# Even and odd tokens in separate halves: a hybrid decoder block whose products read their streamed operand interleaved

## The chip, the cores and the metric

The kernel runs on one core of one Trainium2 chip. The metric is the device time of one execution in microseconds. Three runs of the kernel before the change are given, with their median; one further execution was taken by the hardware profiler.

## The reference

One decoder layer over 256 tokens of width 1024 in float32: two attention branches of 8 heads of 64 (MoBA with rotated queries and keys, FoX with a forget gate), merged by per-channel sigmoid gates, an output projection, then a gated feed-forward part with a causal convolution over three tokens. With 256 tokens MoBA has one block, so both branches are plain causal attention.

```python
h = rms_norm(x, attn_norm_g)
proj = h @ w_in                       # q, k, v of both branches, forget logits, 2 x 1024 gate logits
o_a = merge_heads(moba_attention(qa, ka, va))
o_b = merge_heads(forgetting_attention(qb, kb, vb, log_f))
br_a = o_a @ w_branch_moba            # 512 -> 1024
br_b = o_b @ w_branch_fox             # 512 -> 1024
gates = sigmoid(g_logit + b_gate)
merged = gates[:, :, 0] * br_a + gates[:, :, 1] * br_b
x = x + merged @ w_out                # 1024 -> 1024
h2 = rms_norm(x, ffn_norm_g)
u, g = split(h2 @ w_ffn_up)           # 1024 -> 2 x 2816
g = causal_depthwise_conv(g, ffn_conv_w, ffn_conv_b)
x = x + (silu(g) * u) @ w_ffn_down    # 2816 -> 1024
```

## The kernel before, in words

Everything lies transposed: channels on the 128 partitions, the 256 tokens along the free dimension. A tile such as `oh` is 128 x 8 x 256: eight blocks of 128 channels, each a row of 256 tokens per partition, 4 bytes each.

**Products in three terms.** Every large product is made of reduced fp32 operands (`F32R`). A weight is split into `whi` (its rounded copy, ScalarE, L124) and `wlo` (the rest, VectorE, L125); an activation likewise into a high tile and a low tile. Each 128x128 piece of weight then takes three matmuls: high weight by high activation, high weight by low activation, low weight by high activation. In the products behind attention, and in the gates, the weight piece is the stationary operand and the activation the moving (streamed) one: 256 columns, one for each token, and 256 columns of a PSUM bank as the result.

**The stages, in order on TensorE** (its order is written out by hand):

1. The projections to queries, keys and values (`project`, L222). There the activations `xh` and `xl` are stationary, and 512 columns of weight are streamed. Attention's smaller work (transposes L395, `values` L406) and the eight gate chunks (`gate`, which calls `twin`, L430 to L432, with `xh` and `xl` streamed) are woven between them.
2. `values` makes each pair of heads' output in PSUM and splits it into `oh` (ScalarE, L408) and `ol` (VectorE, L409).
3. The branch products (`wb`, L527 to L529) stream `oh` and `ol`. Their results are multiplied by the gates and added (L533, L534), and split into `mh` (L535) and `ml` (L536), which take the buffers of `xh` and `xl`.
4. The output product (`wo`, L553 to L555) streams `mh` and `ml`; the sum with x is split into `hh` (L561) and `hl` (L562), in the buffers of `oh` and `ol`. The squares for the second norm go to GpSimd and back (L566 to L569, L580).
5. Feed-forward: `up(f)` for 22 chunks streams `hh` and `hl` through `twin` (L430 to L432). It scales the result (L583), runs the convolution (L587 to L589), the SiLU (ScalarE, L590) and the product with u (VectorE, L591) into the halves `sl` and `av` of a work tile, and splits that into `ah` (L595) and `al` (L596), in buffers named qA, qB and kA. `down(p)` (L614 to L616) streams `ah` and `al` of two chunks; it runs one pair of chunks behind `up`. The last one adds x (L620) and sends the output (L621).

Weights come on SyncE's queue, 1 MB at a time, into three `raw` buffers (`load`, L120); `use` asks for the split of a half chunk five halves ahead, in six pairs of `whi` and `wlo`.

Of the kernel before, what the change touches and what calls it, by code (L numbers as in the profile page):

```python
# [8 lines left out]
F32 = mybir.dt.float32  # L9
F32R = mybir.dt.float32r  # L10
BF16 = mybir.dt.bfloat16
AF = mybir.ActivationFunctionType
ALU = mybir.AluOpType
# [5 lines left out]
S = 256  # L19
NT = 2  # L20
D = 1024
KT = D // P
# [19 lines left out]
def decoder_block(ctx, tc, a, out):  # L42
    nc = tc.nc
# [139 lines left out]
    def rsqrt_mean(dst, ss, n, shape, tag):  # L183

        w = T([P, 3] + shape, tag, 2)
        v, y, t = w[:, 0], w[:, 1], w[:, 2]
        nc.vector.tensor_scalar(v, ss, 1.0 / n, EPS, op0=ALU.mult, op1=ALU.add)
        nc.scalar.activation(t, v, AF.Ln)
        nc.scalar.activation(y, t, AF.Exp, scale=-0.5)
        nc.vector.scalar_tensor_tensor(t, v, -0.5, y, op0=ALU.mult, op1=ALU.mult)  # L190
        nc.vector.tensor_tensor(t, t, y, op=ALU.mult)
        nc.vector.scalar_tensor_tensor(dst, t, 1.5, y, op0=ALU.add, op1=ALU.mult)

    rs = T([P, NT], "rs")
    rope = []
# [162 lines left out]
    oh = T([P, KT, S], "oh", 1, F32R)  # L358
    ol = T([P, KT, S], "ol", 1, F32R)
# [39 lines left out]
    def values(br, pair):  # L399
        pT = probs.pop((br, pair))  # L400
        op = bank()
        for i, c in enumerate((slice(0, 256), slice(256, 384))):
            for j in range(2):
                o = HD * j
                vc = br * W4 + (2 * pair + j) * HD
                nc.tensor.matmul(op[o:o + HD, i * P:S], V[:, i, vc:vc + HD], pT[:, j, c], start=(i == 0), stop=(i == 1))  # L406
        b = 4 * br + pair
        nc.scalar.activation(oh[:, b], op[:, 0:S], AF.Copy)  # L408
        nc.vector.tensor_tensor(ol[:, b], op[:, 0:S], oh[:, b].bitcast(F32), op=ALU.subtract)  # L409


    gates = lt[:, :, S:].rearrange("p k (b t) -> p k b t", b=2)
# [5 lines left out]
            nc.tensor.matmul(rp[:, t * P:(t + 1) * P], rs[:, t:t + 1].to_broadcast([P, P]), ident, start=True, stop=True)  # L418
        nc.vector.tensor_copy(rsB, rp[:, 0:S])

    def twin(kind, c, dst, mh, ml):

        for h in range(2):
            wh, wl = use((kind, c), h)
            for i in range(2):
                o = dst[:, i * S:(i + 1) * S]
                for k4 in range(4):
                    k = 4 * h + k4
                    w = slice(k4 * 256 + i * P, k4 * 256 + (i + 1) * P)
                    nc.tensor.matmul(o, wh[:, w], mh[:, k], start=(k == 0 and i == 0), stop=False)  # L430
                    nc.tensor.matmul(o, wh[:, w], ml[:, k], start=False, stop=False)  # L431
                    nc.tensor.matmul(o, wl[:, w], mh[:, k], start=False, stop=(k == KT - 1 and i == 1))  # L432

    def gate(c):
        gp = bank()
# [81 lines left out]
    mh = T([P, KT, S], "xh", 1, F32R)  # L517
    ml = T([P, KT, S], "xl", 1, F32R)
    for c in range(4):
        bp = banks()  # L520
        for br in range(2):
            wh, wl = use(("wb", c), br)
            for j in range(2):
                o = bp[j][:, br * S:(br + 1) * S]
                for k in range(4):
                    w = slice(k * 256 + j * P, k * 256 + (j + 1) * P)
                    nc.tensor.matmul(o, wh[:, w], oh[:, 4 * br + k], start=(k == 0), stop=False)  # L527
                    nc.tensor.matmul(o, wh[:, w], ol[:, 4 * br + k], start=False, stop=False)  # L528
                    nc.tensor.matmul(o, wl[:, w], oh[:, 4 * br + k], start=False, stop=(k == 3))  # L529
        for j in range(2):  # L530
            b = 2 * c + j
            m2 = T([P, 2, S], "sq", 2)
            nc.vector.tensor_tensor(m2, bp[j].rearrange("p (b t) -> p b t", b=2), gates[:, b], op=ALU.mult)  # L533
            nc.vector.tensor_tensor(m2[:, 0], m2[:, 0], m2[:, 1], op=ALU.add)  # L534
            nc.scalar.activation(mh[:, b], m2[:, 0], AF.Copy)  # L535
            nc.vector.tensor_tensor(ml[:, b], m2[:, 0], mh[:, b].bitcast(F32), op=ALU.subtract)  # L536


    hh = T([P, KT, S], "oh", 1, F32R)
    hl = T([P, KT, S], "ol", 1, F32R)  # L540
    acc = [bank() for _ in range(4)]
    x1 = xT
    sqs = T([P, S], "sqs")
    for c in range(4):
        for h in range(2):
            wh, wl = use(("wo", c), h)
            j = 2 * (c % 2) + h
            for i in range(2):
                o = acc[j][:, i * S:(i + 1) * S]
                for k4 in range(4):  # L550
                    k = 4 * (c // 2) + k4
                    w = slice(k4 * 256 + i * P, k4 * 256 + (i + 1) * P)
                    nc.tensor.matmul(o, wh[:, w], mh[:, k], start=(k == 0 and i == 0), stop=False)  # L553
                    nc.tensor.matmul(o, wh[:, w], ml[:, k], start=False, stop=False)  # L554
                    nc.tensor.matmul(o, wl[:, w], mh[:, k], start=False, stop=(k == KT - 1 and i == 1))  # L555
            if c >= 2:
                xx = x1[:, 2 * j:2 * j + 2]
                nc.vector.tensor_tensor(xx, acc[j].rearrange("p (b t) -> p b t", b=2), xx, op=ALU.add)
                for b in (2 * j, 2 * j + 1):
                    g = col(C_G2 + b)  # L560
                    nc.scalar.activation(hh[:, b], x1[:, b], AF.Copy, scale=g)  # L561
                    nc.vector.scalar_tensor_tensor(hl[:, b], x1[:, b], g, hh[:, b].bitcast(F32), op0=ALU.mult, op1=ALU.subtract)  # L562
                sq = T([P, 2, S], "sq", 2)
                nc.scalar.activation(sq, xx, AF.Square)
                if j == 0:
                    nc.gpsimd.tensor_tensor(sqs, sq[:, 0], sq[:, 1], op=ALU.add)  # L566
                else:
                    nc.gpsimd.tensor_tensor(sqs, sqs, sq[:, 0], op=ALU.add)
                    nc.gpsimd.tensor_tensor(sqs, sqs, sq[:, 1], op=ALU.add)  # L569
# [5 lines left out]

    def up(f):
        up_ = bank()
        twin("wu", f, up_, hh, hl)
        if f == 0:
            nc.tensor.matmul(sp[:, 0:S], ones, sqs, start=True, stop=True)  # L580
            rsqrt_mean(rs2, sp[:, 0:S], D, [S], "pT")
        ev = T([P, 2, S], "sq", 2)
        nc.vector.tensor_tensor(ev, up_.rearrange("p (b t) -> p b t", b=2), rs2[:, None, :].to_broadcast([P, 2, S]), op=ALU.mult)  # L583
        u, g = ev[:, 0], ev[:, 1]
        w = T([P, 3, S], "s", 3)
        cv, sl, av = w[:, 0], w[:, 1], w[:, 2]
        nc.scalar.activation(cv, g, AF.Identity, scale=col(C_CW + 2 * NF + f), bias=col(C_CB + f))  # L587
        nc.vector.scalar_tensor_tensor(cv[:, 1:], g[:, 0:S - 1], col(C_CW + NF + f), cv[:, 1:], op0=ALU.mult, op1=ALU.add)
        nc.vector.scalar_tensor_tensor(cv[:, 2:], g[:, 0:S - 2], col(C_CW + f), cv[:, 2:], op0=ALU.mult, op1=ALU.add)  # L589
        nc.scalar.activation(sl, cv, AF.Silu)  # L590
        nc.vector.tensor_tensor(av, u, sl, op=ALU.mult)  # L591
        if f % 2 == 0:
            acts[f // 2] = T([P, 4, S], ("qA", "qB", "kA")[f // 2 % 3], 1, F32R)
        ah, al = acts[f // 2][:, f % 2], acts[f // 2][:, 2 + f % 2]
        nc.scalar.activation(ah, av, AF.Copy)  # L595
        nc.vector.tensor_tensor(al, av, ah.bitcast(F32), op=ALU.subtract)  # L596
# [4 lines left out]
    def down(p):  # L601
        ac = acts.pop(p)
        last = p == NF // 2 - 1
        w2 = [use(("wd", p), h) for h in range(2)]
        order = [(h, d) for d in ((0, 1), (2, 3), (4, 5), (6,), (7,)) for h in range(2)] if last else [(h, (d,)) for h in range(2) for d in range(KT)]
        for h, ds in order:
            wh, wl = w2[h]
            ah, al = ac[:, h], ac[:, 2 + h]
            for d in ds:
                b = 4 if d == 7 else d // 2  # L610
                c = d % 2 if d < 6 else 0
                o = acc[b][:, c * S:(c + 1) * S]
                w = slice(d * P, (d + 1) * P)
                nc.tensor.matmul(o, wh[:, w], ah, start=(p == 0 and h == 0 and c == 0), stop=False)  # L614
                nc.tensor.matmul(o, wh[:, w], al, start=False, stop=False)  # L615
                nc.tensor.matmul(o, wl[:, w], ah, start=False, stop=(last and h == 1 and d == ds[-1]))  # L616
            if last and h == 1:
                n = len(ds)
                y = yy[:, ds[0]:ds[0] + n]
                nc.vector.tensor_tensor(y, acc[b][:, 0:n * S].rearrange("p (b t) -> p b t", b=n), x1[:, ds[0]:ds[0] + n], op=ALU.add)  # L620
                nc.sync.dma_start(out[:, ds[0]:ds[0] + n], y)  # L621
# [75 lines left out]
```

## Time and profile before

| | us |
|---|---|
| three runs | 377.33, 384.51, 383.91 |
| median | 383.91 |
| profiled execution: span from the first to the last instruction | 376.7 |
| TensorE busy in it | 368.5 (98%) |
| VectorE busy | 286.6 (76%) |
| ScalarE busy | 228.0 (61%) |
| GpSimd busy | 16.8 (4%) |
| HBM read | 66.60 MB, 180 GB/s over the span |

The profiled execution has no time of its own besides its span; the fastest run lies 0.6 us above that span and the median run 7.2 us. The granted TensorE clock is 0.999 of full speed.

A row of a group gives line, engine, operation, the tiles it writes and reads, shapes and count, then busy time, the mean duration of one in ns, and the idle time before it with what ended it. Matmuls are pipelined: one lasts longer than the step from its start to the next one's start, and it is the step that counts. The timeline gives start and duration in us.

### The profile page before, as it was taken

The page shows a single profiled execution, that of the slowest core. Times are in us where ns is not written, and L with a number is a line of the kernel's source. Part 1 is how long each engine was busy: PE and PEld are TensorE (multiplying, and loading weights), DVE is VectorE, ACT ScalarE, POOL GpSimd, SP SyncE. Part 2 cuts the span into 40 slices and gives each one's busy share as a digit, 9 for nine tenths or more (in the row PEclk, how much of TensorE's full clock was granted, in tenths as well). Part 3 has the DMA queues.
Part 4 walks back from the last instruction along what each step waited for, and adds up shares of the span by engine and source line. Part 5 has one row for each costly group of instructions (what it writes and reads, how often), then busy time and mean ns, then how long its engine had stood idle before and what let it go on. Part 6 is the DMA issues. An engine that isn't in the chain of part 4 may idle for free.

```text
span 376.7 us, 7085 instructions
## 1 busy us (share of the span) xinstructions
PE 368.5 (98%) x2893; PEld 347.0 (92%) x2893; DVE 286.6 (76%) x504; ACT 228.0 (61%) x382; POOL 16.8 (4%) x19
## 2 busy tenths in 40 slices
PE   7999999999999999999999999999999999999995
PEld 3788887879999999999999999999999999999995
DVE  3979989899997664786787978677686867778653
ACT  4947698659957794545578756464655545455520
POOL 2420000000000000000070000000000000000000
PEclk9999999999999999999999999999999999999999
DMA  7966521735265433545554645564455455545003
GB/s 310 384 254 225 224 113 34 303 130 208 110 215 176 171 113 118 218 161 182 217 172 164 225 171 179 211 222 175 171 216 208 162 197 217 202 151 210 2 0 111
DMA packets 11232, 68.11 MB, mean 181 GB/s; under 512 B 1464, under 2 KB 2624, under 8 KB 3648
## 3 DMA queue, kind: packets, MB, share of 16 engines
q1 hardware_dynamic: 10896, 66.60, 48.7%
q10 hardware_dynamic: 304, 1.06, 0.7%
q8 instruction: 22, 0.36, 0.4%
q14 instruction: 10, 0.08, 0.1%
HBM read 66.60 MB, written 1.06 MB: 180 GB/s over the span
## 4 chain that ended last, share of the span: by engine, by line
PE 79%; ACT 8%; DVE 7%; DMA 3%; issue 1%; POOLq 0%; POOL 0%; SPq 0%; ACTq 0%
PE bank L432 13%; PE bank L430 13%; PE bank L431 13%; PE bank L222 10%; PE bank L616 5%; PE bank L615 5%; PE bank L614 5%; DVE wlo L125 2%; ACT whi L124 2%; PE bank L527 2%; PE bank L528 2%; PE bank L529 2%; DMA lead<-in_lead 2%; ACT qA L273 1%; DMA raw<-in_wg 1%; PE bank L554 1%
## 5 line engine op out<-in xcount | busy, mean ns | idle before, releaser
L125 DVE TENSOR_TENSOR wlo<-raw,whi 128x1024 fp32r<-128x1024 f32 x118 | 146.2, 1243 | 47.2 <-ACT whi L124 47.1
L124 ACT ACTIVATE whi<-raw 128x1024 fp32r<-128x1024 f32 x118 | 124.1, 1057 | 81.7 <-PE bank L431 46.8
L431 PE MATMUL bank<-ol,whi 128*128 128x256 f32 x352 | 97.3, 276 | 0.1
L430 PE MATMUL bank<-oh,whi 128*128 128x256 f32 x352 | 97.4, 277 | 0.0
L432 PE MATMUL bank<-oh,wlo 128*128 128x256 f32 x352 | 97.2, 276 | 0.0
L431 PEld LDWEIGHTS bank<-ol,whi 128*128 128x128 f32 x352 | 66.1, 188 | 0.3 <-DVE ol L562 0.3
L430 PEld LDWEIGHTS bank<-oh,whi 128*128 128x128 f32 x352 | 66.1, 188 | 0.0
L432 PEld LDWEIGHTS bank<-oh,wlo 128*128 128x128 f32 x352 | 66.1, 188 | 0.0
L430 PE MATMUL bank<-xh,whi 128*128 128x256 f32 x128 | 36.2, 283 | 0.0
L432 PE MATMUL bank<-xh,wlo 128*128 128x256 f32 x128 | 35.9, 280 | 0.0
L431 PE MATMUL bank<-xl,whi 128*128 128x256 f32 x128 | 35.9, 280 | 0.0
L222 PE MATMUL bank<-whi,xh 128*128 128x512 f32 x96 | 30.5, 399 | 1.2 <-ACT whi L101 1.2
L222 PE MATMUL bank<-wlo,xh 128*128 128x512 f32 x96 | 30.2, 395 | 0.5 <-DVE wlo L102 0.5
L222 PE MATMUL bank<-whi,xl 128*128 128x512 f32 x96 | 29.8, 391 | 0.0
L432 PEld LDWEIGHTS bank<-xh,wlo 128*128 128x128 f32 x128 | 24.4, 190 | 0.0
L430 PEld LDWEIGHTS bank<-xh,whi 128*128 128x128 f32 x128 | 24.1, 188 | 0.2 <-DVE bias L355 0.2
L431 PEld LDWEIGHTS bank<-xl,whi 128*128 128x128 f32 x128 | 24.1, 188 | 0.0
L222 PEld LDWEIGHTS bank<-wlo,xh 128*128 128x128 f32 x96 | 17.7, 188 | 5.6 <-DVE wlo L102 1.9
L222 PEld LDWEIGHTS bank<-whi,xh 128*128 128x128 f32 x96 | 17.2, 188 | 5.2 <-ACT whi L101 2.1
L222 PEld LDWEIGHTS bank<-whi,xl 128*128 128x128 f32 x96 | 18.0, 188 | 4.1
L583 DVE TENSOR_TENSOR sq<-bank,rs 128x512 f32<-128x512 f32 x22 | 15.1, 690 | 6.5 <-PE bank L432 6.5
L381 ACT ACTIVATE s<-s,nm 128x128 f32<-128x128 f32 (+1 forms) x32 | 14.2, 448 | 8.3 <-DVE nm L378 8.3
(173 smaller groups left out, 768.4 us busy)
## 6 DMA issues: line engine op xcount, KB each, us to landing
raw<-in_wu SPq DMA_DIRECT2D x22, 1024.0 KB, 4.8
raw<-in_wd SPq DMA_DIRECT2D x11, 1024.0 KB, 4.8
raw<-in_qkv SPq DMA_DIRECT2D x9, 1024.0 KB, 4.8
raw<-in_wg SPq DMA_DIRECT2D x8, 1024.0 KB, 4.9
raw<-in_wb SPq DMA_DIRECT2D x4, 1024.0 KB, 4.8
raw<-in_wo SPq DMA_DIRECT2D x4, 1024.0 KB, 4.8
lead<-in_lead SPq DMA_DIRECT2D x3, 768.0 KB, 7.8
raw<-in_qkv SPq DMA_DIRECT2D x2, 512.0 KB, 10.7
```

What stands on the lines that cost most here:

```text
L124: nc.scalar.activation(hi, raw, AF.Copy)
L125: nc.vector.tensor_tensor(lo, raw, hi.bitcast(F32), op=ALU.subtract)
L222: nc.tensor.matmul(pt[t], lhs[:, k, t * P:(t + 1) * P], rhs, start=(k == 0 and i == 0), stop=(k == KT - 1 and i == 2))
L381: last_exp[:] = [nc.scalar.activation(s[:, j, c], s[:, j, c], AF.Exp, scale=-1.0, bias=nm[:, j, i:i + 1], accum_out=l[:, j, i:i + 1])]
L430: nc.tensor.matmul(o, wh[:, w], mh[:, k], start=(k == 0 and i == 0), stop=False)
L431: nc.tensor.matmul(o, wh[:, w], ml[:, k], start=False, stop=False)
L432: nc.tensor.matmul(o, wl[:, w], mh[:, k], start=False, stop=(k == KT - 1 and i == 1))
L527: nc.tensor.matmul(o, wh[:, w], oh[:, 4 * br + k], start=(k == 0), stop=False)
L583: nc.vector.tensor_tensor(ev, up_.rearrange("p (b t) -> p b t", b=2), rs2[:, None, :].to_broadcast([P, 2, S]), op=ALU.mult)
L614: nc.tensor.matmul(o, wh[:, w], ah, start=(p == 0 and h == 0 and c == 0), stop=False)
L615: nc.tensor.matmul(o, wh[:, w], al, start=False, stop=False)
L616: nc.tensor.matmul(o, wl[:, w], ah, start=False, stop=(last and h == 1 and d == ds[-1]))
```

## The change

Three views of a row of 256 tokens are added. `evens` lists a row in natural order as even tokens first, then odd ones. `halves` splits a row that is kept in that new order into its two runs of 128. `pairs` reads such a row back in natural order: token 0 from the first half, token 1 from the second, token 2 from the first, and so on; neighbouring elements of this view lie 128 elements, 512 bytes, apart.

The tiles `oh`, `ol`, `mh`, `ml`, `hh`, `hl`, `sl`, `av`, `ah` and `al` now keep even tokens in front of odd ones. Whoever writes them first reads its source with a step of two elements (`evens`) and writes two runs of 128 (`halves`). Every matmul that streams them reads with `pairs`, so the results in PSUM have their tokens in natural order as before. The gates and the projections keep the old layout. No instruction is added, removed or moved: on each engine the order of instructions and their waits are those of before. Tiles, buffers and transfers are unchanged too.

```diff
+    def evens(ap):
+        return ap.rearrange("p (t a) -> p a t", a=2)
+    def pairs(ap):
+        return ap.rearrange("p (a t) -> p t a", a=2)
+    def halves(ap):
+        return ap.rearrange("p (a t) -> p a t", a=2)
...
-        nc.scalar.activation(oh[:, b], op[:, 0:S], AF.Copy)
-        nc.vector.tensor_tensor(ol[:, b], op[:, 0:S], oh[:, b].bitcast(F32), op=ALU.subtract)
+        nc.scalar.activation(halves(oh[:, b]), evens(op[:, 0:S]), AF.Copy)
+        nc.vector.tensor_tensor(halves(ol[:, b]), evens(op[:, 0:S]), halves(oh[:, b].bitcast(F32)), op=ALU.subtract)
...
-    def twin(kind, c, dst, mh, ml):
+    def twin(kind, c, dst, mh, ml, order=lambda ap: ap):
...
-                    nc.tensor.matmul(o, wh[:, w], mh[:, k], start=(k == 0 and i == 0), stop=False)
-                    nc.tensor.matmul(o, wh[:, w], ml[:, k], start=False, stop=False)
-                    nc.tensor.matmul(o, wl[:, w], mh[:, k], start=False, stop=(k == KT - 1 and i == 1))
+                    rh, rl = order(mh[:, k]), order(ml[:, k])
+                    nc.tensor.matmul(o, wh[:, w], rh, start=(k == 0 and i == 0), stop=False)
+                    nc.tensor.matmul(o, wh[:, w], rl, start=False, stop=False)
+                    nc.tensor.matmul(o, wl[:, w], rh, start=False, stop=(k == KT - 1 and i == 1))
...
+                    rh, rl = pairs(oh[:, 4 * br + k]), pairs(ol[:, 4 * br + k])
...
-            nc.scalar.activation(mh[:, b], m2[:, 0], AF.Copy)
-            nc.vector.tensor_tensor(ml[:, b], m2[:, 0], mh[:, b].bitcast(F32), op=ALU.subtract)
+            nc.scalar.activation(halves(mh[:, b]), evens(m2[:, 0]), AF.Copy)
+            nc.vector.tensor_tensor(halves(ml[:, b]), evens(m2[:, 0]), halves(mh[:, b].bitcast(F32)), op=ALU.subtract)
...
-                    nc.tensor.matmul(o, wh[:, w], mh[:, k], start=(k == 0 and i == 0), stop=False)
+                    nc.tensor.matmul(o, wh[:, w], pairs(mh[:, k]), start=(k == 0 and i == 0), stop=False)
...
-                    nc.scalar.activation(hh[:, b], x1[:, b], AF.Copy, scale=g)
+                    nc.scalar.activation(halves(hh[:, b]), evens(x1[:, b]), AF.Copy, scale=g)
...
-        twin("wu", f, up_, hh, hl)
+        twin("wu", f, up_, hh, hl, pairs)
...
-        nc.scalar.activation(sl, cv, AF.Silu)
-        nc.vector.tensor_tensor(av, u, sl, op=ALU.mult)
+        nc.scalar.activation(halves(sl), evens(cv), AF.Silu)
+        nc.vector.tensor_tensor(halves(av), evens(u), halves(sl), op=ALU.mult)
...
-            ah, al = ac[:, h], ac[:, 2 + h]
+            ah, al = pairs(ac[:, h]), pairs(ac[:, 2 + h])
```

More of the change, by code (lines that the diff above doesn't have):

```diff
@@ L526, in decoder_block @@
                     w = slice(k * 256 + j * P, k * 256 + (j + 1) * P)
-                    nc.tensor.matmul(o, wh[:, w], oh[:, 4 * br + k], start=(k == 0), stop=False)
-                    nc.tensor.matmul(o, wh[:, w], ol[:, 4 * br + k], start=False, stop=False)
-                    nc.tensor.matmul(o, wl[:, w], oh[:, 4 * br + k], start=False, stop=(k == 3))
+                    rh, rl = pairs(oh[:, 4 * br + k]), pairs(ol[:, 4 * br + k])
+                    nc.tensor.matmul(o, wh[:, w], rh, start=(k == 0), stop=False)
+                    nc.tensor.matmul(o, wh[:, w], rl, start=False, stop=False)
+                    nc.tensor.matmul(o, wl[:, w], rh, start=False, stop=(k == 3))
         for j in range(2):
@@ L552, in decoder_block @@
                     w = slice(k4 * 256 + i * P, k4 * 256 + (i + 1) * P)
-                    nc.tensor.matmul(o, wh[:, w], mh[:, k], start=(k == 0 and i == 0), stop=False)
-                    nc.tensor.matmul(o, wh[:, w], ml[:, k], start=False, stop=False)
-                    nc.tensor.matmul(o, wl[:, w], mh[:, k], start=False, stop=(k == KT - 1 and i == 1))
+                    nc.tensor.matmul(o, wh[:, w], pairs(mh[:, k]), start=(k == 0 and i == 0), stop=False)
+                    nc.tensor.matmul(o, wh[:, w], pairs(ml[:, k]), start=False, stop=False)
+                    nc.tensor.matmul(o, wl[:, w], pairs(mh[:, k]), start=False, stop=(k == KT - 1 and i == 1))
             if c >= 2:
@@ L560, in decoder_block @@
                     g = col(C_G2 + b)
-                    nc.scalar.activation(hh[:, b], x1[:, b], AF.Copy, scale=g)
-                    nc.vector.scalar_tensor_tensor(hl[:, b], x1[:, b], g, hh[:, b].bitcast(F32), op0=ALU.mult, op1=ALU.subtract)
+                    nc.scalar.activation(halves(hh[:, b]), evens(x1[:, b]), AF.Copy, scale=g)
+                    nc.vector.scalar_tensor_tensor(halves(hl[:, b]), evens(x1[:, b]), g, halves(hh[:, b].bitcast(F32)), op0=ALU.mult, op1=ALU.subtract)
                 sq = T([P, 2, S], "sq", 2)
```

## The prediction

> **What bounds the kernel now.** I read the page's first lines and the chain that ended last, then the stages, then single matmul steps.
>
> ```profile
> span 376.7 us, 7085 instructions
> PE 368.5 (98%) x2893; PEld 347.0 (92%) x2893; DVE 286.6 (76%) x504; ACT 228.0 (61%) x382; POOL 16.8 (4%) x19
> PE 79%; ACT 8%; DVE 7%; DMA 3%; issue 1%; POOLq 0%; POOL 0%; SPq 0%; ACTq 0%
> ```
>
> TensorE (PE) is busy for 98% of the span and makes 79% of the chain. An average hides stages, so here are the stretches that the change touches: branch products, output product, feed-forward (columns: stretch, then busy time and count for each engine, granted clock, DMA share, GB/s).
>
> ```profile
> core 0: us, PE busy (x) PEld busy (x) DVE busy (x) ACT busy (x) POOL busy (x), PEclk, DMA share, GB/s
> 153.00:175.00 22.00, 22.00 (x196) 22.00 (x196) 19.80 (x33) 11.23 (x16) 0.00 (x0) 1.00 0.47 163
> 175.00:196.00 21.00, 20.88 (x183) 20.68 (x183) 15.44 (x19) 13.81 (x20) 5.86 (x6) 1.00 0.55 194
> 196.00:372.00 176.00, 175.53 (x1547) 175.28 (x1546) 126.69 (x177) 92.50 (x130) 1.76 (x2) 1.00 0.47 170
> ```
>
> Of these 219 us TensorE is idle for 0.6 us, at full granted clock. VectorE (DVE) and ScalarE (ACT) have room and DMA is half used. So what sets the time there is the matmul's step from start to start. How many of them the change touches:
>
> ```profile
> L430 PE MATMUL bank<-oh,whi 128*128 128x256 f32 x352 | 97.4, 277 | 0.0
> L431 PE MATMUL bank<-ol,whi 128*128 128x256 f32 x352 | 97.3, 276 | 0.1
> L432 PE MATMUL bank<-oh,wlo 128*128 128x256 f32 x352 | 97.2, 276 | 0.0
> L527 PE MATMUL bank<-oh,whi 128*128 128x256 f32 x64 | 17.8, 278 | 0.0
> L553 PE MATMUL bank<-xh,whi 128*128 128x256 f32 x64 | 17.7, 276 | 0.0
> L614 PE MATMUL bank<-qA,whi 128*128 128x256 f32 x64 | 17.7, 276 | 0.0
> L614 PE MATMUL bank<-qB,whi 128*128 128x256 f32 x64 | 17.7, 276 | 0.0
> L614 PE MATMUL bank<-kA,whi 128*128 128x256 f32 x48 | 13.2, 276 | 0.0
> ```
>
> ```profile
> L527 PE MATMUL bank<-oh,whi x64: 276/276/385, 147.7 to 169.3; 128*128 128x256 f32 x64
> ```
>
> The last row gives the first start of all of them, 147.7 us. Each of these lines stands for one of three terms with equal counts: 3 x (352 + 64 + 64 + 176) = 1968 matmuls of 256 columns, all waiting for almost nothing (the last column of the groups). Their step, and that of two other kinds, from the timeline of TensorE (start, duration of the merged row, line, tiles, count):
>
> ```profile
> 365.73 0.28 PE L614 MATMUL bank<-qA,whi 128*128 128x256 f32 x1
> 365.84 0.28 PE L615 MATMUL bank<-qA,whi 128*128 128x256 f32 x1
> ...
> 372.42 0.28 PE L616 MATMUL bank<-qB,wlo 128*128 128x256 f32 x1
> ```
>
> ```profile
> 40.03 0.62 PE L222 MATMUL bank<-wlo,xh 128*128 128x512 f32 x2
> ...
> 43.24 0.62 PE L222 MATMUL bank<-whi,xl 128*128 128x512 f32 x2
> ```
>
> ```profile
> 129.73 0.28 PE L432 MATMUL bank<-xh,wlo 128*128 128x256 f32 x1
> ...
> 132.20 0.28 PE L432 MATMUL bank<-xh,wlo 128*128 128x256 f32 x1
> ```
>
> Between the first and the last row of the first fence lie 59 steps: 6.69 us / 59 = **113.4 ns** for 256 columns. In the second, seven rows of two matmuls each: 3.21 us / 14 = 229.3 ns for 512 columns. Twice the columns takes twice the time (0.443 and 0.448 ns a column), with nothing fixed left over: the step is the streaming of columns, not issue, and not the weight load, which is the same 128 columns in both. The third fence (gates, same shape as the first, 21 steps) has 117.6 ns: tiles and surroundings alone move a step by 4.2 ns.
>
> **The change part by part.** No instruction is added, removed or moved, so there are two things to price: what the streamed read costs, and what the writers cost.
>
> *The streamed read.* Before, neighbouring columns are neighbouring words of 4 bytes. After, each column lies 512 bytes from the one before, forth and back. No row of this trace has such a streamed operand, so the cost is bounded.
>
> From below: the read is as fast wherever the word lies. Then nothing changes but the surroundings, which are worth 4.2 ns a step by the gates' row, either way: 1968 x 4.2 ns = 8.3 us. A gain beyond that is not to be had from a read that already takes words in order.
>
> From above: the slowest columns that TensorE takes anywhere in this trace are those of the probabilities' transposes, in the chain of waits:
>
> ```profile
> 125.10 0.81 PE bank L395 x6
> ```
>
> 0.81 us / (6 x 128) = 1.05 ns a column. At that rate 256 columns take 270 ns, 157 ns more than now: 1968 x 157 ns = 308 us.
>
> Between them I take the price of a read that fetches one word at a time. At 0.443 ns a column TensorE takes words more than twice as fast as any other engine here. ScalarE and VectorE by their slopes:
>
> ```profile
> L125 DVE TENSOR_TENSOR wlo<-raw,whi 128x1024 fp32r<-128x1024 f32 x118 | 146.2, 1243 | 47.2 <-ACT whi L124 47.1
> L124 ACT ACTIVATE whi<-raw 128x1024 fp32r<-128x1024 f32 x118 | 124.1, 1057 | 81.7 <-PE bank L431 46.8 <-PE bank L615 7.5 <-PE bank L554 7.4
> L101 ACT ACTIVATE whi<-lead 128x512 fp32r<-128x512 f32 x8 | 5.0, 619 | 1.9 <-DMA lead<-in_lead 1.9
> L102 DVE TENSOR_TENSOR wlo<-lead,whi 128x512 fp32r<-128x512 f32 x8 | 5.5, 684 | 0.1
> ```
>
> ScalarE: (1057 - 619) / 512 = 0.86 ns a word. VectorE: (1243 - 684) / 512 = 1.09 ns. My reading is that TensorE gets its rate by taking at least two neighbouring words in one access, and that in the interleaved row each access yields one useful word. Two ways to price that. Twice today's step: 226.8 ns. One word each 0.86 ns, the best single-word rate in the trace: 219 ns. I take the middle, **223 ns**, 109.5 ns more than now: 1968 x 109.5 ns = **+215.5 us**. This value is nearer to the upper row than to the lower, because the chosen pattern is the worst one for a read of neighbours: no two successive words are adjacent.
>
> The Trainium skill speaks against this change: "SBUF — State Buffer", section "Specifications (TRN2)", has lines of 16 bytes and asks for at least two hits on a line for full bandwidth. In the old order a line would be hit four times running, in the new one once; the page gives no price, and no run so far shows it.
>
> *The writers.* 46 ScalarE and 46 VectorE instructions of 256 words (8 each at L408/L409, L535/L536, L561/L562, 22 each at L590/L591) now read with a step of two words and write two runs. The low half also reads the high tile in two runs. Nothing if a step of two is free. If each word cost twice, 256 x 0.86 = 220 ns on ScalarE and 256 x 1.09 = 279 ns on VectorE: 10.1 and 12.8 us in all. In the three stretches VectorE is busy 161.9 of 219 us and ScalarE 117.5, so TensorE's own work hides both; and the longer TensorE takes, the better. One seam is open, from the output product to the first `up`, where the last two blocks of `hh` and `hl` are written while TensorE has nothing else; before, it waited there once:
>
> ```profile
> L431 PEld LDWEIGHTS bank<-ol,whi 128*128 128x128 f32 x352 | 66.1, 188 | 0.3 <-DVE ol L562 0.3
> ```
>
> With the cover gone, two blocks cost at most 2 x (220 + 279) ns = 1.0 us. I take 0.
>
> *What moves with it.* Weight splits (L124, L125) and the transfers behind them are asked for by the matmuls five halves ahead, so they only get more slack; the same bytes spread over a longer time. The first 147 us and the last 4 us (the output's last additions and transfers) keep their length.
>
> *The sum.* 376.7 + 215.5 = 592.2 us of span. The runs shown lie 0.6 to 7.8 us above the profiled span, the median 7.2 us. So **599 us** is the time to compare with 383.91.
>
> **The rivals.**
>
> *The stream does not care (not slower).* TensorE's reader generates each column's address anyway, and memory gives one word from any address in 0.443 ns. For it: the step is exactly proportional to columns, with no sign of grouping. Against it: no other engine here gets a word faster than 0.86 ns. Span 376.7 us within 8.3 us for the surroundings, plus up to 1.0 us at the seam: 384 us as the runs are timed. It decides if the step stays below 117 ns, 2% of the whole being 7.7 us or 3.9 ns a step. The skill's page "TensorE: Matmul & The Clock Gate", section "Back-to-back issue gap", is this rival: its gap N / 2.4 + 2.5 ns knows only the number of columns. It gives 109 ns for 256 columns and 216 for 512, where the trace has 113.4 and 229.3; it would leave the time as it is.
>
> *Read-ahead hides half.* If accesses overlap, so that a change of place costs half a column's time, the step is 1.5 x 113.4 = 170 ns: +56.7 ns, 1968 x 56.7 = +111.6 us, 488 us of span, 495 us as timed. For it: weights load beside the stream, so the memory has more than one access in flight. Against it: nothing in the trace shows a rate between.
>
> *Worse than double.* If each access waits for the one before it, the transposes' 1.05 ns a column holds: 376.7 + 308 + 7.2 = 692 us. For it: TensorE does run at that rate somewhere. Against it: transposes are another operation, with a weight load for every 128 columns, twice as many as the products have for theirs, and that may be their bound.
>
> *Faster.* Alternating between two places could keep the stream out of the way of the weight load and win what the gates lose, 4.2 ns a step: 368 us of span, 376 timed. Nothing speaks for it but that 113.4 and 117.6 ns differ.
>
> **How the numbers follow.** Double or about it 0.65; half hidden 0.12; worse than double 0.06; no change 0.15; faster 0.02. The time is that of the likeliest, 599 us. The likeliest case by itself spans 219 to 227 ns a step, which is 592 to 607 us as timed (span plus 7.2). The range leaves out no change and faster (0.17) and half of the heavy case (0.03): from 450 us, below the half-hidden 495, to 660 us, a step of 252 ns, between double and the transposes' rate. Faster by over 2% 0.02, within 2% 0.15, slower by over 2% 0.83; 2% is about what a measurement of this kernel can tell from no change.
>
> **What would show it.** The step in `up` and `down` should be 219 to 227 ns and that of the gates still 117.6, in the same trace. The stretch from the first branch product (147.7 us) to the last matmul should grow from 225 to about 440 us, with TensorE still without idle time and granted clock still 1.00. VectorE's and ScalarE's waits for TensorE should grow by as much. The writers' durations show whether a step of two words costs anything; up to double, it changes no total. I am wrong if the step stays under 117 ns (the reader doesn't group words), or if it grows but VectorE or DMA ends the waits (then the stream wasn't the price).

## The result and the profile after

| | before | changed |
|---|---|---|
| median of the runs, us | 383.91 (five, 377.33 to 384.51) | 373.49 (five, 373.19 to 374.80) |
| ratio, 95% interval | | 0.9906 (0.9886 to 0.9927) |
| profiled span, us | 376.7 | 371.9 |

The change makes the kernel faster by 0.7 to 1.1%. The forecast was 599 us. The ratio compares undisturbed runs; three of the five executions of the kernel before took about 384 us, none of the changed kernel did, and these three are left out, which is why the ratio is nearer to 1 than the two medians are.

The page after, the lines that answer to those of before:

```profile
span 371.9 us, 7085 instructions
PE 365.0 (98%) x2893; PEld 344.3 (93%) x2893; DVE 287.9 (77%) x504; ACT 230.6 (62%) x382; POOL 15.5 (4%) x19
PE 90%; ACT 4%; DVE 3%; DMA 1%; issue 0%; SPq 0%; ACTq 0%
```

TensorE is as busy as before, at the same count of instructions. The step of the changed matmuls, from the timeline of TensorE after (`down`, now L625 to L627):

```profile
361.76 0.28 PE L626 MATMUL bank<-qA,whi 128*128 128x256 f32 x1
...
367.56 0.28 PE L627 MATMUL bank<-qB,wlo 128*128 128x256 f32 x1
```

52 steps lie between these rows: 5.80 us / 52 = 111.5 ns, where before had 113.4. Taken over each stage, from the starts of all its matmuls, the step is 111.7 ns in each of the four, against 113.3 before. Unrounded the difference is 1.67 ns (113.33 against 111.66): 1968 x 1.67 ns = 3.3 us. The stretch itself:

```profile
L538 PE MATMUL bank<-oh,whi x64: 275/275/377, 146.5 to 167.7; 128*128 128x256 f32 x64
L627 PE MATMUL bank<-qB,wlo x64: 275/275/275, 228.5 to 367.6; 128*128 128x256 f32 x64
```

From the first branch product to the last matmul it takes 221.1 us, and took 224.7 (147.7 to 372.4): 3.6 us less, of which the step explains 3.3. The other 1.2 us of the span lie ahead of the stretch, in work that the change leaves alone. A second execution of the changed kernel, shown below, starts its branch products at 148.0 us instead of 146.5, so nothing shows that these 1.2 us come from the change.

The writers (ScalarE, then VectorE, each pair in the order of the program):

```profile
L417 ACT ACTIVATE oh<-bank 128x256 fp32r<-128x256 f32 x8 | 2.9, 368 | 0.1
L418 DVE TENSOR_TENSOR ol<-bank,oh 128x256 fp32r<-128x256 f32 x8 | 3.4, 419 | 0.1
L546 ACT ACTIVATE xh<-sq 128x256 fp32r<-128x256 f32 x8 | 3.7, 485 | 1.0 <-DVE sq L545 1.0
L547 DVE TENSOR_TENSOR xl<-sq,xh 128x256 fp32r<-128x256 f32 x8 | 3.4, 442 | 0.0
L601 ACT ACTIVATE s<-s 128x256 f32<-128x256 f32 x22 | 10.5, 482 | 4.6 <-DVE s L600 4.6
L602 DVE TENSOR_TENSOR s<-sq,s 128x256 f32<-128x256 f32 x22 | 9.6, 440 | 1.6 <-ACT s L601 1.6
```

Those that read SBUF with a step of two words became longer: by 75 and 77 ns on ScalarE (410 and 405 before) and by 23 and 21 ns on VectorE (419 before). The pair between them in the program (L572, L573, not shown) also reads SBUF: 588 ns, 88 more, on ScalarE and 672 ns, 14 more, on VectorE. The first pair reads PSUM with the same step and did not change (370 and 419 before). TensorE waits for these at one seam only, below.

### The profile page after: what moved, and what is told of

Its sections match the earlier page's. It is cut to its first block, busy times and chain, and to the rows that moved or that the text cites. A ratio compares the mean times of both kernels' runs of the same rounds, so it can differ in the third digit from the quotient of the medians.

```text
span 371.9 us, 7085 instructions
## 1 busy us (share of the span) xinstructions
PE 365.0 (98%) x2893; PEld 344.3 (93%) x2893; DVE 287.9 (77%) x504; ACT 230.6 (62%) x382; POOL 15.5 (4%) x19
## 4 chain that ended last, share of the span: by engine, by line
PE 90%; ACT 4%; DVE 3%; DMA 1%; issue 0%; SPq 0%; ACTq 0%
PE bank L441 14%; PE bank L440 14%; PE bank L442 14%; PE bank L231 13%; PE bank L625 5%; PE bank L626 5%; PE bank L627 5%; PE bank L538 2%; PE bank L539 2%; PE bank L540 2%; PE bank L415 2%; PE bank L565 2%; PE bank L564 2%; PE bank L566 2%; PE bank L404 2%; DMA lead<-in_lead 1%
## 5 line engine op out<-in xcount | busy, mean ns | idle before, releaser
L441 PEld LDWEIGHTS bank<-ol,whi 128*128 128x128 f32 x352 | 67.6, 192 | 0.7 <-DVE ol L573 0.7
L440 PEld LDWEIGHTS bank<-oh,whi 128*128 128x128 f32 x352 | 67.6, 192 | 0.0
L442 PEld LDWEIGHTS bank<-oh,wlo 128*128 128x128 f32 x352 | 67.6, 192 | 0.0
```

The source lines that it names most:

```text
L440: nc.tensor.matmul(o, wh[:, w], rh, start=(k == 0 and i == 0), stop=False)
L441: nc.tensor.matmul(o, wh[:, w], rl, start=False, stop=False)
L442: nc.tensor.matmul(o, wl[:, w], rh, start=False, stop=(k == KT - 1 and i == 1))
```

## The experiments

A step below is the mean from one matmul's start to the next one's within a stage, from the timeline, without the few that wait. Every kernel changes the kernel before unless said otherwise. First, which half of the change makes the gain.

**Reads alone.**

```diff
+    def order_(ap):
+        return ap.rearrange("p (a t) -> p t a", a=2)
...
-                    nc.tensor.matmul(o, wh[:, w], oh[:, 4 * br + k], start=(k == 0), stop=False)
+                    nc.tensor.matmul(o, wh[:, w], order_(oh[:, 4 * br + k]), start=(k == 0), stop=False)
```

> Writers as before, tiles in natural order; the four groups of products read them with the interleaved view, so the tokens of each product come out permuted and the output is not the reference's. Theory A (the streamed read alone makes the gain): the step of the 1968 matmuls is 111.6 ns as in the changed kernel, against 113.4 before; span about 372 us. Theory B (the writers' order makes it): the step stays 113.4 ns and the span 376 to 377 us.

Step 111.7 ns in all four stages, span 373.9 us (the kernel before had 376.9 to 377.4 us on that chip).

**Writers alone.** `pairs` of the change returns its argument.

> Writers as in the change, even tokens in front, but the products stream the rows as they lie; tokens come out permuted and the output is not the reference's. Theory A (the streamed read alone makes the gain): step 113.4 ns, span 376 to 378 us, ScalarE's writers 70 to 80 ns longer each as in the change. Theory B (the writers): step 111.6 ns, span about 372 us.

Step 113.3 ns, span 377.2 us. Timed as whole kernels the two are not clear of noise (ratios 0.984, from 0.967 to 1.001, and 1.0025, from 0.992 to 1.009); the steps decide. The gain belongs to the streamed read; the writers cost nothing that shows. One expectation missed: the writers are not as long as in the change. L546 and L601, 485 and 482 ns there, take 428 and 423 here, and VectorE's are at 419 as before.

```profile
L546 ACT ACTIVATE xh<-sq 128x256 fp32r<-128x256 f32 x8 | 3.2, 428 | 0.8 <-DVE sq L545 0.8
L601 ACT ACTIVATE s<-s 128x256 f32<-128x256 f32 x22 | 9.2, 423 | 3.9 <-DVE s L600 3.9
```

With the reads alone the same work took 409 and 411 ns. So 18 ns come from the writers' step of two words, and some 57 more only where TensorE streams interleaved at the same time. (L572, not shown, has 500 ns before, 527 with the writers alone and 588 with both.)

**A step of two words, and turns of four words.** In `order_`, `"p (t a) -> p a t"` with a = 2, and `"p (a t r) -> p t a r"` with a = 2, r = 4.

> Before's writers; the products stream each row with a step of two elements (8 bytes), all even tokens, then all odd ones; tokens come out permuted. If any access pattern with two free dimensions shortens the start of a matmul (form theory): step 111.6 ns. If it takes reading from two distant places in turn (place theory): 113.4 ns or more, since this read walks one place at a time, twice as fast. If neighbouring words did matter to the reader: longer by tens of ns.

> Before's writers; the products stream four neighbouring words (16 bytes) from the first half of the row, then four from the second, in turn; tokens come out permuted. Form theory (any pattern with more than one free dimension): 111.6 ns. Place theory (two distant places in turn): near 111.6 ns too if the turn may be every fourth word, 113.4 ns if the turn must be at every word. Longer than 113.4 ns would speak for a cost of each jump.

```profile
299.73 0.42 PE L434 MATMUL bank<-oh,whi 128*128 128x256 f32 x1
...
305.93 0.43 PE L434 MATMUL bank<-oh,whi 128*128 128x256 f32 x1
```

These are two rows of `up` with the step of two words, 27 steps apart: 229.6 ns. Median 606.8 us, more than half again of before. So streaming can cost what the prediction asked for, at a step of only 8 bytes. Turns of four took 126.6 ns, 403.8 us: form theory fell, place theory in its simplest form too.

**Ways, runs and weights.** Since every stage had the same step, each stage now carries another pattern.

```diff
+    def rd_wb(ap):
+        return ap.rearrange("p (a t) -> p t a", a=4)
+    def rd_wo(ap):
+        return ap.rearrange("p (a t) -> p t a", a=8)
```

> Before's writers. Each group of products streams its rows with another number of interleaved places: gates 2 (512 bytes apart), branch products 4 (256 bytes), output product 8 (128 bytes), up 16 (64 bytes), down 64 (16 bytes); tokens come out permuted. Line theory (memory hands over lines of at least 16 bytes, one in the time of four columns, and a few are held): 2 and 4 ways near 112 ns, and from some number of ways on each column costs a line of its own, up to 4 x 107 = 427 ns. Place theory (words fetched together must lie in different sub-memories, chosen by address bits; the step of two words hit only half of them): the step depends on the distance, not on the number of places: 512, 256 and 128 bytes may be alike, 16 bytes is the worst. If the gates' read also falls to 111.6 ns, the gain is of the pattern and not of the stage.

> Before's writers; tokens come out permuted or from a neighbouring block. Branch products: turns of two words from each half; output product: turns of eight words; up: word by word from two places 129 words apart, so the words of a pair have different parity; down: two plain runs of 128 words from two neighbouring blocks. Line theory: all near 112 ns, except that turns of two and eight lie on either side of the 126.6 ns that turns of four took, if the cost is one of the jump (more jumps, more cost: two words dearer than four, eight cheaper). Place theory: 129 words differ from 128. Form theory (any second free dimension shortens the start): down 111.6 ns; otherwise 113.4 ns.

> Parts of the computation are replaced, and the output is not the reference's. Branch products: the stationary operand is every second word of a 256-word slice, plain stream; output product: the same with the stream interleaved as in the change; up: the stationary operand is one column repeated 128 times (next to nothing to read for it), plain stream; down: the streamed operand is one word repeated 256 times, plain weights. Meeting theory (the plain stream loses 16 slots of 0.417 ns a matmul to the weight load, the interleaved one 12): up falls to about 107 ns, and down too. If up stays at 113.4 ns and down falls, the lost slots belong to the stream's own reading. If both stay, they belong to the matmul's start. A weight load with a step of two words should take 107 x 2 = 213 ns and then set the step, if the load has the same port rate as the stream.

Two rows each of `ways`, output product (8 places, 47 steps) and branch products (4 places, 71 steps):

```profile
179.66 0.40 PE L569 MATMUL bank<-xh,whi 128*128 128x256 f32 x1
...
190.00 0.40 PE L571 MATMUL bank<-xh,wlo 128*128 128x256 f32 x1
```

```profile
155.75 0.31 PE L545 MATMUL bank<-oh,wlo 128*128 128x256 f32 x1
...
165.92 0.31 PE L544 MATMUL bank<-ol,whi 128*128 128x256 f32 x1
```

That is 220.0 and 143.2 ns. Sixteen places took 220.0, 64 places 233.2 ns; nothing came near the 427 ns of the line theory. The gates, with two places, took 111.7 ns instead of 116.8. In `runs`, turns of two words took 168 ns, of eight 123 ns, two plain runs 115.5 ns, and two places 129 words apart 111.7 ns. In `weights`, one repeated weight column left the plain stream at 113.4 ns, one repeated streamed word took 111.7 ns, and a weight piece read with a step of two words took 120.0 ns under a plain stream and 118.3 ns under an interleaved one. So the weights' addresses are not what the plain stream loses to (meeting theory fell), and a weight load with a step has nothing of the doubling.

**Distance and places.** The first holds the places at two and varies the distance; the second holds the distance and varies the places. `hand` writes the pattern out as pairs of step and count, the last pair innermost.

```diff
+    def hand(tl, dims, back=0):
+        return bass.AP(tensor=tl.tensor, offset=tl.offset - back, ap=[list(tl.ap[0])] + dims)
...
+    def rd_wo(ap):
+        return hand(ap, [[1, 128], [16, 2]])
```

> Streams are replaced, and the output is not the reference's: each row is read word by word from exactly two places in turn, both walking one word at a time, at distances of 16 bytes (gates), 32 (branch products), 64 (output product), 128 (up) and 256 (down). Holding theory (the reader holds the fetched piece of two places, so that each place still uses what it fetched): 111.7 ns at every distance. Place theory (two words fetched together must lie in sub-memories told apart by an address bit worth 512 bytes or so): about 220 ns below 256 bytes, as with 8, 16 and 64 places at 128, 64 and 16 bytes.

> Streams are replaced, and the output is not the reference's. All places lie 512 bytes or a multiple apart: branch products 4 places, output product 8, up 16, word by word in turn; gates two places in turns of 16 words; down two places 2048 bytes apart that each walk two words at a time. Holding theory: 4 places near the 143 ns that 4 places at 256 bytes took, 8 and 16 near 220 ns, and down near 220 ns, since each fetched pair of words is then used for one. Place theory: 4, 8 and 16 places 111.7 ns as two, because the distance is right. If down takes 112 ns, a fetched piece is longer than two words.

In `distance`, every stage took 111.7 ns, at 16 bytes as at 256: place theory fell. In `places`, 4 places took 143.3 ns, just as at half the distance, 8 took 247 and 16 took 267 ns, turns of sixteen words 120 ns (in the gates, where the plain row takes some 117). Why 8 and 16 places cost more at 512 bytes than the 220 ns that they took at 128 and 64 bytes was not tried. Two rows of `up` with 16 places, 23 steps, 267.0 ns:

```profile
299.65 0.45 PE L438 MATMUL bank<-ol,whi 128*128 128x256 f32 x1
...
305.79 0.45 PE L437 MATMUL bank<-oh,whi 128*128 128x256 f32 x1
```

But `down`, two places that each walk two words at a time, took 113.8 ns. It uses every second word, as the 230 ns read did. Holding theory in the form that was on record (220 ns there) fell with that.

**Parity.** It keeps the words of a step of two and changes only their order.

```diff
-            ah, al = ac[:, h], ac[:, 2 + h]
+            ah, al = hand(ac[:, 0], [[8, 64], [2, 2], [4, 2]], -h), hand(ac[:, 0], [[8, 64], [2, 2], [4, 2]], -512 - h)
```

> Streams are replaced, and the output is not the reference's. Branch products: two places in turn, each walking four words (16 bytes) at a time; output product: two places walking three words; up: every word twice in succession; down: one place, the even words 0, 2, 4, 6 of each eight read in the order 0, 4, 2, 6, so that columns of even number take words 0 and 2 of a 16-byte piece and columns of odd number words 4 and 6 of the next. Two-path theory (columns of even number and of odd number are fetched apart, and each path runs at full rate if it uses every 16-byte piece at least twice in succession): branch products 220 to 250 ns, since each piece serves once; output product between; up 111.7 ns; down 113 to 120 ns although it uses every second word as the 230 ns read did. Piece-count theory (only the number of 16-byte pieces fetched for each column counts): branch products 220 ns or more, down 230 ns as the plain step of two words, whatever the order.

`down` in the order 0, 4, 2, 6 (53 steps) and the branch products with two places that walk four words (45 steps):

```profile
399.79 0.28 PE L621 MATMUL bank<-qA,whi 128*128 128x256 f32 x1
...
405.97 0.28 PE L623 MATMUL bank<-qB,wlo 128*128 128x256 f32 x1
```

```profile
154.67 0.41 PE L534 MATMUL bank<-oh,whi 128*128 128x256 f32 x1
...
164.99 0.41 PE L534 MATMUL bank<-oh,whi 128*128 128x256 f32 x1
```

116.6 and 229.3 ns; walking three words 176 ns; every word twice 111.7 ns. Each is where the two-path theory put it. Piece counting asked for 230 ns in `down` and is out.

**Narrow weights.** Most weight pieces are 64 columns wide.

```diff
-                    nc.tensor.matmul(o, wh[:, w], mh[:, k], start=(k == 0 and i == 0), stop=False)
+                    n = 64 if kind == "wu" and 0 < k < KT - 1 else P
+                    f = rd_wu if kind == "wu" else (lambda ap: ap)
+                    nc.tensor.matmul(o[0:n], wh[:, w][:, 0:n], f(mh[:, k]), start=(k == 0 and i == 0), stop=False)
...
```

> Parts of the products are left out, and the output is not the reference's: most weight pieces in branch products, up and down are only 64 columns wide. Branch products stream one word repeated, up the interleaved row, down the plain row. If 111.7 ns is the weight load's own step (128 columns; 512 interleaved columns took 216 ns, which is 512 slots of 0.417 ns and 6 more, so 256 alone would take 109 ns): narrow ones fall to 109 ns in up and branch products, and stay at 113.3 ns in down. If 111.7 ns is a floor of the matmul: 111.7 ns in up and branch products.

In `up` most steps are 109 ns (mean 109.7 with the wide ones in it), in the branch products 109 to 112 (mean 110.4, half of them wide). So 111.7 ns is the step with 128 weight columns, and an interleaved row of 256 takes 109 with 64. Whether the weight load or the 128 result rows make the difference is not shown, since the edit halves both. The plain row in `down` did not stay at 113.3: its mean went to 118.0 ns, 119 with narrow pieces and 113.3 to 113.7 in the first and last pair, which have wide ones. That alone would point to the weights. But the output product of the same run streams plain rows with full pieces of 128, as before, and it took 117.8 ns instead of 113.3 (51 steps here, 117.6):

```profile
172.28 0.28 PE L559 MATMUL bank<-xh,whi 128*128 128x256 f32 x1
...
178.28 0.28 PE L559 MATMUL bank<-xh,whi 128*128 128x256 f32 x1
```

So a plain row can fall to the longer step with nothing narrowed beside it.

**Interleaving elsewhere.** Two versions add to the change; both compute the reference. The first has the host's layout put even columns first in each block of 512 projection weights and streams them with `pairs`; the second also streams the gates so and puts the tokens back in order where VectorE takes the gates' result from PSUM (L437 of the kernel before).

```diff
-                rh, rl = wh[:, k2 * 512:(k2 + 1) * 512], wl[:, k2 * 512:(k2 + 1) * 512]
+                rh, rl = pairs(wh[:, k2 * 512:(k2 + 1) * 512]), pairs(wl[:, k2 * 512:(k2 + 1) * 512])
...
-        twin("wg", c, gp, xh, xl)
+        twin("wg", c, gp, xh, xl, pairs)
```

> The change, and the projections to queries, keys and values stream their weight columns interleaved as well (the columns of each block of 512 come from memory with the even ones in front, so no engine does more work). If interleaving saves a fixed 4 slots of 0.417 ns a matmul: 288 x 1.7 = 0.5 us, span 371.4 us. If it saves by the column or by the collisions that the 512-column steps show (226 to 232 ns against 213): up to 288 x 10 ns = 2.9 us, span 369 us. If 512 columns are too far apart to be interleaved: no less than the change's 371.9 us.

> The change, the projections' weight columns interleaved, and the gates' stream read interleaved too, straight from the natural rows, with the tokens put back in order where VectorE takes the result from PSUM. Gates: 111.7 ns a step instead of 116.8 on average, 384 x 5.1 = 2.0 us; the projections as in the run before this one (216 ns a step). Span 369 to 370 us. If the projections or attention wait for splits instead, less: 371 us.

> The change itself once more, beside the next kernel on one chip: span 371.5 to 374 us, 1 to 2.5% below the kernel before.

> The kernel with interleaved reads in projections and gates too, beside the change on one chip. If the shorter steps (gates 384 x 5 ns, projections 288 x 13 ns, 5.6 us in all) come through: 366 to 368 us. If projections and attention are paced by the splits of weights and by softmax instead, it stands within 1 us of the change, with TensorE's waits before 140 us longer by what the steps saved.

A projection matmul now takes 216 ns, not 229. Rows of `everywhere_again`, 16 steps, 3.45 us:

```profile
37.78 0.59 PE L231 MATMUL bank<-wlo,xh 128*128 128x512 f32 x2
...
41.23 0.59 PE L231 MATMUL bank<-whi,xh 128*128 128x512 f32 x2
```

With the projections alone the span was 371.5 us, 0.9866 of before (0.9787 to 0.9945), little below the change's 371.9 on another chip: of the 288 x 13 ns = 3.7 us that these steps save, little shows in the span, where 369 us was forecast for such a saving. With the gates it came to 371.3 us on one chip and 371.0 us on the next, where the change itself had 373.3. There the medians are 373.21 and 375.16 us, the ratios to before 0.9847 (0.9811 to 0.9884) and 0.9901 (0.9873 to 0.9928). So it beats the kernel before, and the change by about 0.5% (six runs of each; the two intervals overlap a little). Both forecasts for the span of `everywhere_again` missed: 366 to 368 us was too low, and within 1 us of the change too near. The first branch product of the two on that chip, the change first:

```profile
L538 PE MATMUL bank<-oh,whi x64: 275/275/377, 148.0 to 169.2; 128*128 128x256 f32 x64
```

```profile
L538 PE MATMUL bank<-oh,whi x64: 275/275/377, 144.2 to 165.4; 128*128 128x256 f32 x64
```

Here 3.8 us of the 5.6 us that the steps save arrive. One pair of traces is not enough for that figure: the first trace of this kernel (`everywhere`) starts its branch products at 146.1 us and the first of the change at 146.5, so 0.4 us arrive there (two chips). TensorE's waits in `everywhere_again` show where the rest went:

```profile
PE bank L381 <- DVE kA L288: 1.9, 2, 1.3
PE bank L231 <- ACT whi L101: 1.8, 1, 1.8
...
PE bank L591 <- POOL sqs L580: 0.6, 1, 0.6
```

The change had 0.7 and 0.8 us at the first two and none at the third. The wait for the split of the keys (L288) is the one that grew each time: 1.6 to 1.9 us in the three traces with interleaved projections, 0.7 in both of the change. The wait for the first weights' split (L101) goes from 0.3 to 1.8 us over those three traces, and was 1.2 in the kernel before. The wait for the sum of the squares (L580) makes the stretch behind longer here, 222.5 us against 221.0, but `everywhere` has none of it and the kernel before has 0.5 us. So the wait for the keys' split takes back a part of the gain in every trace; the other two come and go between executions.

## Why the prediction was wrong

**What bounds the kernel** was right: TensorE's step, proportional to columns, with no wait that matters. Faster steps made a shorter kernel, 3.3 us of steps giving 3.6 us of the stretch.

**The streamed read** is the step that failed: "TensorE gets its rate by taking at least two neighbouring words in one access, and that in the interleaved row each access yields one useful word", priced at 223 ns. It takes 111.7. The price was near for a read of single words, and the pattern was the wrong one for it: reads of one row with a step of two words, of 8, 16 or 64 places, and of two places walking four words take 220 to 233 ns (247 and 267 when the 8 and 16 places lie 512 bytes apart), at the 219 to 227 forecast or a little above. That a middle between twice the step and ScalarE's rate came so near is luck as far as the runs go: none ties TensorE's read to another engine's rate. What was false is that neighbouring in the order of columns is what counts.

The runs fit this: columns of even number and columns of odd number are fetched on two paths. Each keeps the full rate if it uses a piece of 16 bytes at least twice before it goes on. The plain row gives each path two words of each piece (113.3 ns). Two interleaved rows give each path its own row and four words of each piece (111.7). A step of two words gives one (230); the same words in the order 0, 4, 2, 6 give two (116.6). With a step of four in two rows it is one again (229.3), and with three it lies between (176). The two paths and the 16 bytes are an inference from these steps, the smallest found that fits them; no counter shows them. Other patterns it does not fit in size. Taken literally it asks for about 220 ns with four places in turn and with turns of two words, where a path leaves each piece after one word; they took 143 and 168 ns. With turns of four, eight and sixteen words it asks for the plain row's step; they took 126.6, 123 and 120 ns. So going back to a piece and jumping between rows have prices of their own, which were not measured apart.

The Trainium skill, "SBUF — State Buffer", section "Specifications (TRN2)", was cited against this change. Its two hits on a 16-byte line for full bandwidth fit the runs if they are counted for each path and not for the stream: read over the stream, as the prediction did, it gives the wrong sign here. By the same rule a step of two fp32 words in one row should be free, two hits a line; the run has 230 ns, and the measurement decides.

**"No change"**, the rival at 0.15, was nearest in time. Its reason, that the reader gives one word from any address in 0.443 ns, fell with the step of two words. The **faster** rival named a gain from keeping the stream out of the way of the weight load, down to 368 us of span. The way was right and the size under half: 3.6 us in the stretch of the 8.3, and 1.67 of the 4.2 ns a step. The reason is not shown: one repeated weight column left the plain row at 113.4 ns. The other two rivals, half hidden and worse than double, did not occur. The second rested on a misreading: the 0.81 us of six transposes holds the tail of the last one, and their starts lie 109 ns apart after the first (166 ns), 0.85 ns a column and not 1.05. At that rate 256 columns take 218 ns, so the bound from above lay no higher than the price that was taken.

**Where the small gain comes from.** The plain row loses a little in its own reading: one repeated word streams at 111.7 ns, like the interleaved row. It can lose more. The gates' plain row has two steps, for stretches of some microseconds each, in one profile, here of the change:

```profile
105.11 0.28 PE L442 MATMUL bank<-xh,wlo 128*128 128x256 f32 x1
...
109.19 0.28 PE L442 MATMUL bank<-xh,wlo 128*128 128x256 f32 x1
...
110.22 0.28 PE L440 MATMUL bank<-xh,whi 128*128 128x256 f32 x1
...
111.98 0.28 PE L440 MATMUL bank<-xh,whi 128*128 128x256 f32 x1
```

36 steps of 113.3 ns, eight small matmuls, then 15 of 117.3. Interleaved, the gates have 111.7 throughout. Why the plain row has two steps, and what switches it, stays open. Narrow weights went with 119 ns in `down`, but the output product of the same run had 117.8 with full weights, so a part of the weight load in it is not shown.

**The writers** came out inside their bounds (up to 88 ns on ScalarE and 23 on VectorE, 220 and 279 allowed) and hidden as said. That most of it appears only beside the interleaved stream was not foreseen. At the **seam** into `up` TensorE waits a little longer for the writers, as the open cover there allowed:

```profile
L441 PEld LDWEIGHTS bank<-ol,whi 128*128 128x128 f32 x352 | 67.6, 192 | 0.7 <-DVE ol L573 0.7
```

0.7 us against 0.3, within the 1.0 that was set. The seam as a whole did not get longer: before, TensorE also waited 0.5 us there for the sum of the squares (L580), and in this trace after it does not. **The front and the tail** were to keep their length; the front was 1.2 us shorter in one trace and 0.3 us longer in the next, with nothing changed in it. The **range** excluded the likeliest alternative on the strength of an order of words that no row of the trace had shown.

## What to carry to other kernels

Before pricing a streamed operand's layout, ask which words the columns of even and of odd number take: two contiguous streams taken in turn are free, and here 1.5% a matmul better than one, while one stream with a step of two words doubles the time. A price bounded only by other engines' rates says nothing of the pattern, so a forecast resting on it should keep "no change" inside its range. A shorter matmul step pays only where TensorE alone sets the pace: 3.3 us of it came through whole behind attention, and 0.4 and 3.8 of 5.6 us ahead of it in two pairs of traces.

## What the runs showed of the hardware

- Streaming 256 fp32r columns: 111.7 ns for two places in turn that each walk one word at a time, 113.3 or 117.3 to 117.8 plain, 143 for four places, 220 to 267 for eight or more, 230 for a step of 8 bytes. For 512 columns: 216 interleaved, 229 plain.
- With 128 weight columns no stage here has a mean step below 111.7 ns; with 64 it reaches 109. A weight piece read with a step of two words adds only 6 to 7 ns.
- A step of two words from SBUF adds 18 to 27 ns to a ScalarE instruction of 256 words and nothing to VectorE's while TensorE streams plain rows, 75 to 88 and 14 to 23 ns while it streams interleaved ones; from PSUM it adds nothing to either. Why the two add up so was not tried.
